# One adaLN block, two gate blocks and the compression summed on TensorE's column groups

## The chip, the cores and the metric

The kernel runs on 1 core of a Trainium2 chip. The metric is the device time of one execution, in microseconds (us). Engines are called PE (TensorE, its weight loads PEld), DVE (VectorE), ACT (ScalarE), POOL (GpSimd) and SP (SyncE, which here only starts DMAs). Each has its own in-order queue of instructions.

## The reference, cut to what matters

One layer over 256 tokens of width 4096. What the change touches is the vector-matrix product `mod` and the function `compress`:

```
mod = c @ w_ada[l] + b_ada[l]                      # c: 4096, w_ada: 4096 x 12288
shift, scale, gate = jnp.split(mod, 3, axis=-1)
u = x * (1.0 + scale[:, None]) + shift[:, None]
proj = u @ w_in[l]                                 # 256 x 4096 times 4096 x 11824
...
def compress(k, pe, w1, w2):                       # k: kc or vc, 256 tokens, 2 groups of 128
    blk = k[:, cmp_idx] + pe[:, None, :]           # 15 windows of 32 tokens, stride 16
    blk = ...reshape(B, n_cmp, G, CMP_LEN * D)     # 32 * 128 = 4096 inputs
    return jax.nn.silu(blk @ w1) @ w2              # w1: 4096 x 256, w2: 256 x 128
...
y = jnp.concatenate([y_rg, y_nsa, y_hg], axis=-1) @ w_out[l]
x = _layer_norm(ALPHA * x + (1.0 + gate[:, None]) * y, ln_g[l], ln_b[l])
```

Between `proj` and `y` stand three groups of heads: a gated recurrence (rg), sparse attention with compressed, selected and window branches (nsa), and a gated linear recurrence in chunks (hg).

## The kernel before, in words

All weights are float32 and are streamed once from HBM, in tiles of 128 x 1024 (512 KB). PE multiplies the large matrices as three products of rounded parts (a weight tile `raw` is split into `hi` on ACT and `lo` = raw - hi on DVE and POOL), lines 457 (input projection, "win" steps) and 969 (output projection, "wout" steps). Small products are made from unrounded float32 operands; each of these stands in the trace as two passes through PE.

**Stages.** The 4096 inputs are cut into ten blocks of 2, 2, 2, 3, 3 and five times 4 tiles of 128. For each block, `mod` has to be there for the block's rows (scale and shift), and then its rows of `w_in` are multiplied. So the order is: sum adaLN block 0; then for each block kb its win steps, while the chunks of adaLN block kb+1 arrive and are summed. In the last block's win steps the heads' values become complete, and the heads' own work begins. After them come the wout steps, in three parts; the first part needs for each of its 8 column blocks the head pairs 0 to 3 (rg) and 12 (hg), in this order.

**The sum of an adaLN or gate block.** A chunk is 128 partitions x 2 rows x 512 columns, from tile pool `raw`/`hi`/`lo`/`ra` (four buffers each; after the start only `ra`). `ada_sum` (line 352) takes the oldest chunk and for each of its rows lets DVE do ps = raw * c + ps on 128 x 512 (two instructions). At the block's end ACT copies ps to SBUF and PE sums over the partitions with a product with ones (`ada_end` line 395 for scale and shift, `gate_end` line 414 for a gate block of 512 columns). There are ten adaLN blocks and eight gate blocks, numbered NKB to NKB+7; the gate blocks fall due from the last win block on to the wout steps. In the start stage every third chunk of block 0 (5 of 16) is summed by PE instead (`ada_on_pe`, line 368, products at 375): the 128 x 128 piece of the chunk is the weight and one column of c moves, 8 products for a chunk. After block 0 PE runs N_IDLE = 8 idle products (line 1219).

**The compression.** 16 steps "cmp", one in between the win steps of the last block: 8 for kc, then 8 for vc. A step holds 4 of the 32 tokens of a window; for each it makes 2 products (line 511) with a 128 x 128 piece of w1 as weight and 30 moving columns (15 windows x 2 groups). ACT and DVE then make the silu of the sum (`post`).

**What sets the order.** A planner in the kernel writes the order of every engine's queue. It goes through the steps; background work ("fibers": the heads, gate ends, constants) is advanced by `run_bg` (line 1177), one stage of each fiber per call. In the last win block and after it, `run_bg` is called twice in a step: after the first part of the step's products (line 1255 and after) and at its end. `Meter` counts what each of DVE, ACT and POOL owes; `lapse` pays off HALF = 1.28 us for each call; fibers wait while DVE or ACT owes over MAY_OWE. Heads run in lanes of 2 (rg) and 3 (hg, nsa); the hg lane opens when all rg fibers have been started, the nsa lane when all hg fibers have been. When a wout step needs a head pair that isn't written yet, the planner calls `run_bg` again and again until that fiber is complete: all fiber instructions it writes meanwhile stand in the queues ahead of that step. An hg fiber (line 668) goes through seven levels, L = 1 to 64: four small products (line 708), whose result DVE puts into a matrix with copy_predicated, while DVE and POOL scale q and k for the next level.

Of the kernel before, what the change touches and what calls it, by code (L numbers as in the profile page):

```python
# [11 lines left out]
FT = mybir.dt.float32  # L12
# [6 lines left out]
P = 128  # L19
# [115 lines left out]
def trunk(ctx: ExitStack, tc: tile.TileContext, pack, xT, xz, w_ada, b_row, w_in, w_out, rg_w, w1, w2,  # L135
# [68 lines left out]
    def late_consts():  # L204
# [20 lines left out]
        late["cb"] = cb  # L225
        vm = consts.tile([P, 1], FT, name="vm")
# [112 lines left out]
    def ada_begin(b):  # L339
        _, w, m = ADA[b]  # L340
        ada_state[b] = [ps_x() for _ in range(0, w, 512)]

# [9 lines left out]
    def ada_sum():  # L352
        _, b, i, raw, _ = pending.pop(0)
        _, w, m = ADA[b]
        acc = ada_state[b]
        for j in range(m):
            c_ = vec("c", i * m + j)
            for q, ps in enumerate(acc):
                r_ = raw[:, j, q * 512:min(w, (q + 1) * 512)]
                n = r_.shape[-1]  # L360
                if i == 0 and j == 0:
                    dve.tensor_scalar(ps[:, :n], r_, c_, None, op0=OP.mult)
                else:
                    dve.scalar_tensor_tensor(ps[:, :n], r_, c_, ps[:, :n], op0=OP.mult, op1=OP.add)
        if b >= NKB and i == NKT // m - 1:
            fibers.append([gate_end(b - NKB), 1, 0, 0, tick[0] + GATE_WAIT])

    def ada_on_pe(raw, first):

        _, w, m = ADA[0]  # L370
        if first:
            ada_state["pe"] = ps_x()
        for j in range(m):
            for q in range(w // P):
                nc.tensor.matmul(ada_state["pe"][:, q:q + 1], lhsT=raw[0][:, j, q * P:(q + 1) * P],
                                 rhs=vec("c", raw[1] * m + j), start=first and j == 0 and q == 0,
                                 stop=False, skip_group_check=True)

    def ada_end(kb, xt=None):
# [13 lines left out]
        pp = ada_state.pop("pe") if kb == 0 else ps_x()  # L393
        for q in range(2 * n):
            nc.tensor.matmul(pp[:, q:q + 1], lhsT=acc[q], rhs=ones[:, 0:1],  # L395
                             start=kb > 0, stop=True, skip_group_check=kb == 0)
# [103 lines left out]
    def cmp_step(which, c):  # L500
# [3 lines left out]
        def mm():  # L504
# [3 lines left out]
            for i in range(4):  # L508
                l = 4 * c + i
                for hf in range(2):  # L510
                    nc.tensor.matmul(s_["ph"][:, hf * 256:hf * 256 + 2 * N_CMP],
                                     lhsT=st.raw[:, i * 256 + hf * P:i * 256 + (hf + 1) * P],
                                     rhs=s_["kpe"][l // 16][:, l % 16].rearrange("p a b -> p (a b)"),
                                     start=(l == 0 and hf == 0), stop=(l == CMP_LEN - 1 and hf == 1),
                                     skip_group_check=True)
                if i == 1:
                    yield
# [4 lines left out]
        def post():  # L522
# [3 lines left out]
            h_ = consts.tile([P, 2, 2 * N_CMP], FT, name=f"cmp_h{which}")  # L526
            sg = strm.tile([P, 2, 256], FT, name=nm("ev"), tag="ev", bufs=2)
            ph = s_["ph"].rearrange("p (a b) -> p a b", a=2)[:, :, :2 * N_CMP]
            act.activation(sg[:, :, :2 * N_CMP], ph, AF.Sigmoid)
            dve.tensor_mul(h_, ph, sg[:, :, :2 * N_CMP])  # L530
            ps_free()
            drop(2)
            s_["h"] = h_
            done.add(("cmp_h", which))

        st.work.append((mm, post))
        return st

    def cmp_prep(which):
# [4 lines left out]
        for a in range(2):  # L544
            t_ = slot("kpe", [P, 16, 2, N_CMP])
            for g in range(2):
                dve.tensor_add(t_[:, :, g], kv[:, :, g, a:a + N_CMP],
# [679 lines left out]
    for i in range(N):  # L1227
# [94 lines left out]
ON_PE = 3  # L1322
N_IDLE = 8
# [89 lines left out]
```

## Time and profile before

| | us |
|---|---|
| median of 3 runs (lowest, highest) | 1651.84 (1648.28, 1655.22) |
| profiled execution, its own time | 1653.54 |
| its span, first to last instruction | 1651.7 |
| PE busy in the span | 1601.7 (97%), 11800 matmuls |
| PEld, weight loads | 1503.8 (91%) |
| DVE busy | 1327.6 (80%) |
| ACT, POOL busy | 971.5 (59%), 953.7 (58%) |
| DMA read | 485.12 MB, 296 GB/s over the span |

How to read it: a matmul's time in the trace reaches from its start to the end of its run through the array, and several are under way at once. So PE is shown busy even where matmuls start further apart than they could; how far apart they start is the better measure, and a wait shows in the chain of waits or as a stretch with fewer matmuls than the time would allow.

### The profile page before, as it was taken

The page shows a single profiled execution, that of the slowest core. Times are in us where ns is not written, and L with a number is a line of the kernel's source. Part 1 is how long each engine was busy: PE and PEld are TensorE (multiplying, and loading weights), DVE is VectorE, ACT ScalarE, POOL GpSimd, SP SyncE. Part 2 cuts the span into 40 slices and gives each one's busy share as a digit, 9 for nine tenths or more (in the row PEclk, how much of TensorE's full clock was granted, in tenths as well). Part 3 has the DMA queues.
Part 4 walks back from the last instruction along what each step waited for, and adds up shares of the span by engine and source line. Part 5 has one row for each costly group of instructions (what it writes and reads, how often), then busy time and mean ns, then how long its engine had stood idle before and what let it go on. Part 6 is the DMA issues. An engine that isn't in the chain of part 4 may idle for free.

```text
span 1651.7 us, 33249 instructions
## 1 busy us (share of the span) xinstructions
PE 1601.7 (97%) x11800; PEld 1503.8 (91%) x11800; DVE 1327.6 (80%) x2297; ACT 971.5 (59%) x1557; POOL 953.7 (58%) x765
## 2 busy tenths in 40 slices
PE   7999999998999999999999999889999999999997
PEld 7999999998999999999999998889988888878884
DVE  5778988799788788788787787899689688968875
ACT  3887666665655555555555566763565555655552
POOL 2579977786655555455455445567543445455555
PEclk9999999999999999999999998999999999999999
DMA  8998989998999899899898886767667766689983
GB/s 321 377 333 307 373 299 344 306 384 305 335 339 343 292 343 328 301 348 327 300 344 321 316 293 225 252 230 262 236 223 242 240 212 205 217 294 370 341 327 146
DMA packets 146486, 491.50 MB, mean 298 GB/s; under 512 B 16264, under 2 KB 17288, under 8 KB 146320
## 3 DMA queue, kind: packets, MB, share of 16 engines
q1 hardware_dynamic: 146320, 489.38, 82.8%
q8 instruction: 93, 1.52, 0.4%
q14 instruction: 73, 0.60, 0.1%
HBM read 485.12 MB, written 4.19 MB: 296 GB/s over the span
## 4 chain that ended last, share of the span: by engine, by line
PE 81%; DVE 9%; DMA 4%; ACT 3%; issue 2%; POOL 1%; SPq 0%; DVEq 0%; ACTq 0%; POOLq 0%
PE mm L457 51%; PE mm L969 21%; DVE ps L119 2%; DVE lo L119 2%; DMA raw<-in_w_in_dram 2%; DVE acc L119 2%; DMA ra<-in_w_ada_dram 1%; ACT hi L119 1%; DVE rgt L119 1%; PE ps L708 1%; PE ps L395 1%; PE ps L901 1%; PE ps L792 1%; PE ps L1296 1%; DVE hgA L119 1%
## 5 line engine op out<-in xcount | busy, mean ns | idle before, releaser
L119 POOL TENSOR_TENSOR lo<-raw,hi 128x576 fp32r<-128x576 f32 (+4 forms) x527 | 707.8, 1345 | 606.2 <-ACT hi L119 581.2
L119 ACT CAST hi<-raw 128x1024 fp32r<-128x1024 f32 (+3 forms) x527 | 528.8, 1003 | 489.2 <-POOL lo L119 230.2
L457 PE MATMUL mm<-uh,hi 128*128 128x256 f32 x2560 | 718.1, 281 | 15.7 <-DVE lo L119 13.6
L457 PE MATMUL mm<-uh,lo 128*128 128x256 f32 x2560 | 712.5, 278 | 1.7 <-DVE lo L119 1.1
L457 PE MATMUL mm<-ul,hi 128*128 128x256 f32 x2560 | 712.4, 278 | 0.0
L119 DVE SCALAR_TENSOR_TENSOR ps<-ra,pk,ps 128x512 f32<-128x512 f32 x750 | 525.2, 727 | 11.7 <-DMA ra<-in_w_ada_dram 5.8
L457 PEld LDWEIGHTS mm<-uh,hi 128*128 128x128 f32 x2560 | 484.5, 189 | 19.3 <-DVE lo L119 16.5
L457 PEld LDWEIGHTS mm<-uh,lo 128*128 128x128 f32 x2560 | 483.9, 189 | 2.1 <-DVE lo L119 1.3
L457 PEld LDWEIGHTS mm<-ul,hi 128*128 128x128 f32 x2560 | 484.7, 189 | 0.3 <-issue 0.2
L119 DVE TENSOR_TENSOR lo<-raw,ps 128x448 fp32r<-128x448 f32 (+4 forms) x500 | 303.1, 606 | 225.8 <-ACT ps L119 184.5
L119 ACT CAST ps<-raw 128x448 fp32r<-128x448 f32 (+4 forms) x500 | 259.6, 519 | 7.4 <-DVE acc L119 6.4
L119 DVE TENSOR_TENSOR acc<-mm,acc 128x512 f32<-128x512 f32 (+1 forms) x346 | 231.2, 669 | 0.0
L969 PE MATMUL mm<-hi,yh 128*128 128x512 f32 x512 | 210.8, 412 | 0.3 <-ACT ev L119 0.3
L969 PE MATMUL mm<-hi,yl 128*128 128x512 f32 x512 | 201.3, 393 | 0.0
L969 PE MATMUL mm<-lo,yh 128*128 128x512 f32 x512 | 200.1, 391 | 0.0
L969 PEld LDWEIGHTS mm<-hi,yh 128*128 128x128 f32 x512 | 96.4, 188 | 23.3 <-issue 5.7
L457 PE MATMUL mm<-hi,uh 128*128 128x256 f32 (+1 forms) x384 | 110.4, 288 | 7.1 <-ACT hi L119 3.0
L969 PEld LDWEIGHTS mm<-hi,yl 128*128 128x128 f32 x512 | 96.1, 188 | 21.5
L969 PEld LDWEIGHTS mm<-lo,yh 128*128 128x128 f32 x512 | 96.5, 188 | 19.1 <-issue 1.2
L457 PE MATMUL mm<-hi,ul 128*128 128x256 f32 (+1 forms) x384 | 108.9, 284 | 0.0
L457 PE MATMUL mm<-lo,uh 128*128 128x256 f32 (+1 forms) x384 | 108.9, 284 | 0.0
L119 POOL TENSOR_TENSOR acc<-ev,acc 128x512 f32<-128x512 f32 x77 | 101.9, 1323 | 2.4 <-ACT ev L119 2.4
(203 smaller groups left out, 1488.3 us busy)
## 6 DMA issues: line engine op xcount, KB each, us to landing
ra<-in_w_ada_dram SPq DMA_DIRECT2D x324, 512.0 KB, 5.5
raw<-in_w_in_dram SPq DMA_DIRECT2D x291, 512.0 KB, 4.8
raw<-in_w_out_dram SPq DMA_DIRECT2D x128, 512.0 KB, 4.8
raw<-in_w_in_dram SPq DMA_DIRECT2D x90, 384.0 KB, 5.3
ra<-in_w_ada_dram SPq DMA_DIRECT2D x64, 384.0 KB, 5.6
ra<-in_w_dram SPq DMA_DIRECT2D x16, 512.0 KB, 4.2
xz<-in_xz_dram SPq DMA_DIRECT2D x16, 256.0 KB, 5.8
out_dram<-z SPq DMA_DIRECT2D x16, 256.0 KB, 2.4
```

The costliest lines, as they stand in the source:

```text
L119: return f(*a, **k)
L395: nc.tensor.matmul(pp[:, q:q + 1], lhsT=acc[q], rhs=ones[:, 0:1], start=kb > 0, stop=True, skip_group_check=kb == 0)
L457: nc.tensor.matmul(dst, lhsT=l_, rhs=r_, start=s and n_ == 0, stop=e and n_ == 2)
L708: nc.tensor.matmul(pl[:, (2 * x + j) * 64:(2 * x + j + 1) * 64], lhsT=k[:, j, x * P:(x + 1) * P], rhs=qp[:, j, x * P:(x + 1) * P].rearrang ...
L792: nc.tensor.matmul(s1[:, b * T:(b + 1) * T], lhsT=q[:, j, P:], rhs=kk[b][:, g], start=True, stop=True)
L901: nc.tensor.matmul(o, lhsT=v0, rhs=eT[:, 0:2], start=b == 0, stop=False)
L969: nc.tensor.matmul(state[x], lhsT=a_, rhs=b_, start=ci == 0 and j == 0 and n_ == 0, stop=ci == len(part) - 1 and j == 1 and n_ == 2)
L1296: nc.tensor.matmul(pb, lhsT=rows[-1 - x], rhs=rows[i // 2][:, i % 2 * 512:i % 2 * 512 + 512], start=True, stop=True)
```

## The change

Adds: `sel`, a constant of 128 x 32 with ones at rows n, 32+n, 64+n and 96+n of column n. The blocks in ON_PE (adaLN block 0 and the first two gate blocks) get their accumulator set to zero by DVE, and `ada_sum` makes four products for a chunk instead of DVE's two instructions: one column of c is the weight (128 x 1) and 256 columns of the chunk move; the result is one row of 256, at partition 0, 32, 64 or 96 of the accumulator, which are TensorE's four column groups. The ends of the blocks stay as they were: the copy by ACT and the product with ones, which now sums four rows and zeros.

The compression's products are turned round in the same way: 32 columns of the windows' values are the weight (30 and two of zeros), 256 columns of w1 move, and the four tokens of a step go to the four column groups; 4 products in a step instead of 8. The four partial sums are then copied by ACT and added by two products with `sel` in a new fiber, `cmp_hidden`. The planner calls `run_bg` only once in a cmp step now. The idle products are 4 instead of 8.

```diff
+        sel = consts.tile([P, 32], FT, name="sel")
+        dve.tensor_reduce(sel, ident.rearrange("p (a m) -> p m a", a=4), axis=AX.X, op=OP.add)
...
         ada_state[b] = [ps_x() for _ in range(0, w, 512)]
+        if b in ON_PE:
+            dve.memset(ada_state[b][0], 0.0)
...
-        for j in range(m):
+        if b in ON_PE:
+
+            for j in range(2):
+                for h in range(2):
+                    o = 32 * (2 * j + h)
+                    nc.tensor.matmul(acc[0][o:o + 1, h * 256:h * 256 + 256], lhsT=vec("c", i * 2 + j),
+                                     rhs=raw[:, j, h * 256:h * 256 + 256], start=i == 0, stop=i == NKT // 2 - 1,
+                                     skip_group_check=True)
+        for j in range(m if b not in ON_PE else 0):
...
-    def ada_on_pe(raw, first):
...
-                nc.tensor.matmul(ada_state["pe"][:, q:q + 1], lhsT=raw[0][:, j, q * P:(q + 1) * P],
-                                 rhs=vec("c", raw[1] * m + j), start=first and j == 0 and q == 0,
-                                 stop=False, skip_group_check=True)
...
-                for hf in range(2):
-                    nc.tensor.matmul(s_["ph"][:, hf * 256:hf * 256 + 2 * N_CMP],
-                                     lhsT=st.raw[:, i * 256 + hf * P:i * 256 + (hf + 1) * P],
-                                     rhs=s_["kpe"][l // 16][:, l % 16].rearrange("p a b -> p (a b)"),
-                                     start=(l == 0 and hf == 0), stop=(l == CMP_LEN - 1 and hf == 1),
-                                     skip_group_check=True)
-                if i == 1:
-                    yield
+                nc.tensor.matmul(s_["ph"][32 * i:32 * i + 32, :256], lhsT=s_["kpe"][l // 16][:, l % 16],
+                                 rhs=st.raw[:, i * 256:(i + 1) * 256], start=c == 0, stop=c == 7,
+                                 skip_group_check=True)
...
+            s_["part"] = slot("part", [P, 512])
+            act.copy(s_["part"][:, :256], s_["ph"][:, :256])
             ps_free()
             drop(2)
+            fibers.append([cmp_hidden(which), 1, 0, 0, tick[0] + 1])
...
+        for hf in range(2):
+            nc.tensor.matmul(ph[:, 32 * hf:32 * hf + 32], lhsT=s_["part"][:, hf * P:(hf + 1) * P], rhs=late["sel"],
+                             start=True, stop=True)
...
-            t_ = slot("kpe", [P, 16, 2, N_CMP])
+            t_ = slot("kpe", [P, 16, 2 * N_CMP + 2])
+            dve.memset(t_, 0.0)
...
-        if i % ON_PE == ON_PE - 1:
-            raw = ada_load(0, i, tags[i])
-            ada_on_pe((raw, i), i == ON_PE - 1)
-        else:
-            ada_chunk(0, i, 0, tags[i])
-            ada_sum()
+        ada_chunk(0, i, 0, tags[i])
+        ada_sum()
...
-                    if i >= n_win0:
+                    if i >= n_win0 and st.kind != "cmp":
                         lapse(HALF)
                         run_bg()
...
-ON_PE = 3
-N_IDLE = 8
+ON_PE = 0, NKB, NKB + 1
+N_IDLE = 4
```

Three places in PE's queue show what the change does to the order. In the rows, L367 (after) is the new product of `ada_sum`, L375 (before) the old one of `ada_on_pe`; L395 and L398 are the product with ones, L1219 and L1230 the idle products, L457 and L460 the input projection.

First, PE at the end of the start stage, before:

```order
L375 MATMUL ps_97<-pk,lo_150 128x1 x8
L375 MATMUL ps_97<-pk,ra_168 128x1 x8
L395 MATMUL ps_97<-ones,aacc_182 128x1 x4
L1219 MATMUL mm_197<-ident 128x128 x8
L457 MATMUL mm_251<-uh_211,hi_186 128x256
L457 MATMUL mm_251<-ul_212,hi_186 128x256
```

And after:

```order
L367 MATMUL ps_84<-ra_172,pk 1x256 x4
L367 MATMUL ps_84<-ra_178,pk 1x256 x4
L398 MATMUL ps_195<-ones,aacc_184 128x1 x4
L1230 MATMUL mm_200<-ident 128x128 x4
L460 MATMUL mm_250<-uh_210,hi_188 128x256
L460 MATMUL mm_250<-ul_211,hi_188 128x256
```

PE sums 16 chunks there (the last two stand here) instead of 5; the 11 others leave DVE's queue, and four idle products are gone.

Second, PE around the third cmp step in the last win block, before; L511 is the compression's product:

```order
L457 MATMUL mm_14053<-uh_13532,hi_13934 128x256
L457 MATMUL mm_14053<-ul_13533,hi_13934 128x256
L457 MATMUL mm_14053<-uh_13532,lo_13935 128x256
L511 MATMUL ps_13848<-kpe_13684,ra_13968 128x30 x8
L457 MATMUL mm_14137<-uh_13489,hi_14003 128x256
```

And after; L513 is the compression's product, L630 a product of an rg fiber:

```order
L460 MATMUL mm_14063<-uh_13534,hi_13948 128x256
L460 MATMUL mm_14063<-ul_13535,hi_13948 128x256
L460 MATMUL mm_14063<-uh_13534,lo_13949 128x256
L367 MATMUL ps_13403<-ra_13911,pk 1x256 x4
L513 MATMUL ps_13864<-ra_13970,kpe_13690 32x256 x4
L630 MATMUL ps_14118<-rgy_13994,rgw_13992 128x256 x2
L630 MATMUL ps_14121<-rgy_13994,rgw_13992 128x256 x2
L367 MATMUL ps_13403<-ra_13964,pk 1x256 x4
L367 MATMUL ps_13403<-ra_13966,pk 1x256 x4
L460 MATMUL mm_14143<-uh_13491,hi_14015 128x256
```

Gate chunks (L367) now stand in PE's queue, often right beside a cmp step; there are 32 such chunks and 16 cmp steps between the win steps.

Third, PE ahead of the fifth wout step, which needs head pair 12. Before (L969 is the output projection; L756, L742 to L744, L708, L733 and L769 belong to hg fibers):

```order
L969 MATMUL mm_16065<-hi_16038,yl_15365 128x512
L756 MATMUL ps_16174<-ones,hgsq_16131 128x1 x4
L742 MATMUL ps_16180<-hgA_15321,acc_726 128x128
L743 MATMUL ps_16180<-hgA_15322,acc_726 128x128
L744 MATMUL ps_16180<-hgA_15321,acc_726 128x128
...
L708 MATMUL ps_16187<-hgqp_15324,hgk_15214 128x64 x4
L756 MATMUL ps_16209<-ones,hgsq_16199 128x1 x4
...
L969 MATMUL mm_16047<-hi_16079,yh_16235 128x512
```

And after (L984 is the output projection, L723 a level of an hg fiber, L748 to L784 its later products):

```order
L984 MATMUL mm_15913<-hi_15892,yl_15921 128x512
L723 MATMUL ps_16039<-hgqp_15788,hgk_15605 128x64 x4
L723 MATMUL ps_16057<-hgqp_15926,hgk_15835 128x64 x4
L723 MATMUL ps_16062<-hgqp_15603,hgk_15002 128x64 x4
L723 MATMUL ps_16075<-hgqp_15788,hgk_15605 128x64 x4
L723 MATMUL ps_16080<-hgqp_15603,hgk_15002 128x64 x4
L723 MATMUL ps_16089<-hgqp_15926,hgk_15835 128x64 x4
...
L748 MATMUL ps_16228<-hgqp_15926,hgk_15835 128x128 x2
L784 MATMUL ps_16232<-ident,rs_16206 128x128 x4
...
L984 MATMUL mm_15901<-hi_15932,yh_16251 128x512
```

Sixteen levels of three hg fibers stand between the fourth and the fifth wout step, where one stood before. The first product of an hg fiber comes after 8748 of the 10368 large products, and came after 8448. From the place after the 8916th on, the heads' products stand at the same large products as before.

## Rows read from the trace of the kernel before

**Rows 1.** Windows of the core: us, busy (instructions) of each engine, clock, DMA, GB/s.

```profile
core 0: us, PE busy (x) PEld busy (x) DVE busy (x) ACT busy (x) POOL busy (x), PEclk, DMA share, GB/s
440.00:960.00 520.00, 520.00 (x4538) 520.00 (x4537) 413.01 (x683) 288.32 (x400) 270.22 (x193) 1.00 0.90 326
1000.00:1166.00 166.00, 150.60 (x1173) 146.13 (x1172) 153.24 (x239) 93.42 (x143) 103.12 (x85) 0.94 0.71 249
1166.00:1632.00 466.00, 461.15 (x2258) 379.61 (x2257) 365.37 (x657) 269.78 (x484) 237.55 (x188) 1.00 0.73 254
```

**Rows 2.** Waits of PE, whole span: who waited for whom, total, times, longest.

```profile
PE mm L457 <- DVE lo L119: 17.3, 16, 5.0
PE ps L511 <- DMA ra<-in_w_dram: 2.0, 1, 2.0
```

**Rows 3.** The chain that ended last: start, duration, what.

```profile
684.46 126.74 PE mm L457 x1104
...
1147.64 2.62 PE ps L708 x24
...
1153.14 1.70 PE ps L511 x16
```

**Rows 4.** Groups of PE instructions by form, 1000 to 1166 us.

```profile
L511 PE MATMUL ps<-kpe,ra 128*128 128x30 f32 x192 | 24.1, 278 | 2.0 <-DMA ra<-in_w_dram 2.0
L708 PE MATMUL ps<-hgqp,hgk 128*128 128x64 f32 x144 | 18.4, 278 | 1.0 <-DVE hgA L119 1.0
```

**Rows 5.** Groups of DVE instructions by form, 1000 to 1166 us.

```profile
L119 DVE SCALAR_TENSOR_TENSOR ps<-ra,pk,ps 128x512 f32<-128x512 f32 x56 | 42.2, 753 | 1.1
...
L119 DVE COPY_PREDICATED hgA<-mask,ps 128x256 f32<-128x256 int32 x17 | 9.2, 539 | 0.0
L119 DVE TENSOR_TENSOR hgqp<-hgqp,acc 128x256 f32<-128x256 f32 x9 | 7.9, 878 | 0.0
```

**Rows 6.** Timeline of DVE, first instruction of the first and third gate block.

```profile
951.14 0.74 DVE L119 TENSOR_SCALAR ps<-ra,pk 128x512 f32<-128x512 f32 x1
...
1136.97 0.79 DVE L119 TENSOR_SCALAR ps<-ra,pk 128x512 f32<-128x512 f32 x1
```

**Rows 7.** Timeline of the end of the start stage.

```profile
24.13 3.57 PE L375 MATMUL ps<-pk,ra 128*128 128x1 f32 x16 [0.27 <-DMA ra<-in_w_ada_dram]
25.46 1.55 DVE L119 SCALAR_TENSOR_TENSOR ps<-ra,pk,ps 128x512 f32<-128x512 f32 x2 [0.72 <-DMA ra<-in_w_ada_dram]
27.68 1.86 PE L395 MATMUL ps<-ones,aacc 128*128 128x1 f32 x8
29.40 3.76 PE L1219 MATMUL mm<-ident 128*128 128x128 f32 x16
30.89 0.62 ACT L119 CAST uh<-xT 128x512 fp32r<-128x512 f32 x1 [1.88 <-DVE xT L119]
32.82 0.56 PE L457 MATMUL mm<-uh,hi 128*128 128x256 f32 x1
34.77 0.28 PE L457 MATMUL mm<-uh,hi 128*128 128x256 f32 x1
```

**Rows 8.** Timeline of PE around narrow and 256-column float32 products.

```profile
1343.50 0.40 PE L969 MATMUL mm<-hi,yl 128*128 128x512 f32 x1
1343.73 0.60 PE L873 MATMUL ps<-ident,lc 128*15 128x128 f32 x4
1344.09 0.48 PE L969 MATMUL mm<-hi,yh 128*128 128x512 f32 x1
1344.41 0.40 PE L969 MATMUL mm<-lo,yh 128*128 128x512 f32 x1
...
1346.94 0.59 PE L792 MATMUL ps<-acc,acc 128*128 128x256 f32 x2
1347.37 0.38 PE L793 MATMUL ps<-acc,acc 128*128 128x128 f32 x2
```

**Rows 9.** Timeline of PE ahead of the fifth wout step.

```profile
1180.98 0.95 PE L756 MATMUL ps<-ones,hgsq 128*128 128x1 f32 x8
...
1190.58 0.48 PE L969 MATMUL mm<-hi,yh 128*128 128x512 f32 x1
```

More of the change, by code (lines that the diff above doesn't have):

```diff
@@ L225, in late_consts @@
         late["cb"] = cb
+        sel = consts.tile([P, 32], FT, name="sel")
+        dve.tensor_reduce(sel, ident.rearrange("p (a m) -> p m a", a=4), axis=AX.X, op=OP.add)
+        yield 0
+        late["sel"] = sel
         vm = consts.tile([P, 1], FT, name="vm")
@@ L366, in ada_sum @@
             fibers.append([gate_end(b - NKB), 1, 0, 0, tick[0] + GATE_WAIT])
-    def ada_on_pe(raw, first):
[L370 to L374, printed above, removed]
-                nc.tensor.matmul(ada_state["pe"][:, q:q + 1], lhsT=raw[0][:, j, q * P:(q + 1) * P],
-                                 rhs=vec("c", raw[1] * m + j), start=first and j == 0 and q == 0,
-                                 stop=False, skip_group_check=True)
     def ada_end(kb, xt=None):
@@ L392, in ada_end @@
         yield 1
-        pp = ada_state.pop("pe") if kb == 0 else ps_x()
+        pp = ps_x()
         for q in range(2 * n):
             nc.tensor.matmul(pp[:, q:q + 1], lhsT=acc[q], rhs=ones[:, 0:1],
-                             start=kb > 0, stop=True, skip_group_check=kb == 0)
+                             start=True, stop=True)
         yield 0
@@ L525, in post, with cmp_hidden @@
             s_ = CMP[which]
[L526 to L530, printed above, removed]
+            s_["part"] = slot("part", [P, 512])
+            act.copy(s_["part"][:, :256], s_["ph"][:, :256])
             ps_free()
             drop(2)
-            s_["h"] = h_
-            done.add(("cmp_h", which))
+            fibers.append([cmp_hidden(which), 1, 0, 0, tick[0] + 1])
         st.work.append((mm, post))
         return st
+    def cmp_hidden(which):
+        s_ = CMP[which]
+        ph = ps_x()
+        for hf in range(2):
+            nc.tensor.matmul(ph[:, 32 * hf:32 * hf + 32], lhsT=s_["part"][:, hf * P:(hf + 1) * P], rhs=late["sel"],
+                             start=True, stop=True)
+        drop()
+        yield 0
+        h_ = consts.tile([P, 2, 2 * N_CMP], FT, name=f"cmp_h{which}")
+        sg = strm.tile([P, 2, 256], FT, name=nm("ev"), tag="ev", bufs=2)
+        act.activation(sg[:, 0, :64], ph[:, :64], AF.Sigmoid)
+        dve.tensor_mul(h_.rearrange("p a (g n) -> p (a g) n", g=2),
+                       ph[:, :64].rearrange("p (a n) -> p a n", n=16)[:, :, :N_CMP],
+                       sg[:, 0, :64].rearrange("p (a n) -> p a n", n=16)[:, :, :N_CMP])
+        ps_free()
+        s_["h"] = h_
+        done.add(("cmp_h", which))
+        yield 0
     def cmp_prep(which):
@@ L544, in cmp_prep @@
         for a in range(2):
-            t_ = slot("kpe", [P, 16, 2, N_CMP])
+            t_ = slot("kpe", [P, 16, 2 * N_CMP + 2])
+            dve.memset(t_, 0.0)
             for g in range(2):
-                dve.tensor_add(t_[:, :, g], kv[:, :, g, a:a + N_CMP],
+                dve.tensor_add(t_[:, :, 16 * g:16 * g + N_CMP], kv[:, :, g, a:a + N_CMP],
                                pe[:, 16 * a:16 * a + 16, None].to_broadcast([P, 16, N_CMP]))
```

## The prediction

> **What bounds the kernel now.** I read the views in this order: windows, waits of PE, chain, then groups and timeline of the stretches that lose time. The windows [rows 1] show three kinds of stretch. From 440 to 960 us PE is busy without a gap; the chain there is one run of 1104 large products in 126.74 us [rows 3], 0.115 us each, and nothing but PE's own work counts. From 1166 to 1632 PE is busy for 461 of 466 us. In between, from 1000 to 1166, PE has 15 us of plain gaps and a granted clock of 0.94 on average, while DVE is busy for 153 of 166 us: here DVE sets the pace. The waits agree: PE's longest total is for `lo` parts from DVE, 17.3 us [rows 2].
>
> How much that stretch loses I take from the matmul starts. It holds 1173 [rows 1], of which 192 are of the compression and 144 of hg levels [rows 4]. The chain gives 1.70/16 = 0.106 us for the first kind and 2.62/24 = 0.109 for the second [rows 3]. So PE needs 192 x 0.106 + 144 x 0.109 + 837 x 0.115 = 132 us, and some 4 for about 45 changes from one kind of product to another, at 0.09 each: after the narrow products of [rows 8] the next large start follows at 0.32 instead of 0.23. That is 136 of 166 us: **30 us are lost**.
>
> **The change part by part**, for the profiled execution's 1653.5 us.
>
> *Price of four products on four column groups.* The trace has no two products on different groups. It has the pass: a float32 product with 256 moving columns is two passes, 0.43 us together (from 1346.94 to 1347.37 in [rows 8]). A chunk, and a cmp step, is four such products, eight passes. If the groups work at the same time, that is 0.43 us; if not, 1.72. I take 0.6: the two passes, and 0.17 for the time that a pass needs to run out (it lasts 0.39 to 0.40, while the next starts after 0.23 [rows 8]). I choose the low end since the four products share neither rows of the result nor weights; this is the weakest number of the prediction.
>
> The Trainium skill, "TensorE: Matmul & The Clock Gate", Part 3, reports products on three column groups side by side at 2.38 times the speed. No row here shows this; by that factor eight passes would take about 0.72 us, an estimate, and the sum below would be 6 us higher.
>
> *Gate blocks.* Off DVE go 2 blocks x 16 chunks x 2 instructions x 0.753 us [rows 5] = 48 us. They lie between 951 and 1137 us [rows 6], even enough that 137/186 of them, 35 us, fall behind 1000, where DVE is the bound; the first 13 relieve nothing, since PE is full there. DVE's 153 us become about 118 for 166, so PE becomes the bound. Of the 30 lost us I let 6 remain for waits on single results (DMA of a cmp tile, 2.0 [rows 2], ACT): **-24**; bounds -30 and -12. On PE come 32 x 0.6 = **+19**; bounds 14 and 55. The waits for the chunks' DMAs move from DVE's queue to PE's, where large products stand behind them; the planner sums a chunk some steps after its load, so I cost this at nothing, and it is part of the 6.
>
> *Compression.* 16 steps x 1.70 us [rows 3] = 27.2 go; 16 x 0.6 = 9.6 come, with 0.9 for two times eight passes of `cmp_hidden` at 0.109 (4 products): **-17**; bounds -19 and +1. The zeroing of the window tiles and of three accumulators is under 2 us on DVE, hidden once DVE isn't the bound.
>
> *Changes of kind.* The 16 cmp places were there; 32 new places at 0.09: **+3**, less where a chunk stands beside a cmp step.
>
> The Trainium skill, "TensorEngine Tiling (Array Packing)", Key Properties, speaks against the change here: it says that going from one tiling to another drains the array. The nearest rows, products with 15 columns of weights between large ones [rows 8], start 0.23 us after the large one ahead of them, as large ones do among themselves, and cost 0.09 at their end; that is no drain on the way in. What a drain would make of the sum is a rival below.
>
> *Start.* The last chunk of block 0 is there at 25.46 us, since DVE waited until then; DVE ends at 27.01 [rows 7]. On PE it ends at about 26.1. The product with ones takes 1.86 us for 8 passes [rows 7], twice the later spacing, as do the ten large products from 32.82 to 34.77 (0.217 us apart against 0.115): I read that as the lower clock level, with one-column products ahead of it. With 256 columns moving I expect the higher one, 0.9 less in each of the two. The first large product starts at 32.82, though its operand uh was ready at 31.51; the idle products, which end at 33.16, stood in its way [rows 7], and half of them go. So it starts at about 29.9, and up to 3.8 us are gained. From about 160 to 440 us PE waited for DVE's results (about half of the 17.3 of [rows 2]), and part of such a lead may be given back there: **-2.5**; bounds -4 and, if the eight passes go one by one (16 chunks x 1.72 = 27.5 us, from about 6 on), +5.
>
> *What else moves: the hg fibers.* One call of `run_bg` less in each cmp step delays the rg fibers, and the hg lane opens 300 large products later. Its work is then written while the planner is stuck at the fifth wout step: sixteen levels of three fibers, one after the other on PE, with nothing else to run. Before, this place took 9.6 us [rows 9] for 76 passes, 8.3 us of work. After, PE has there 16 x 8 passes and 88 of the fibers' ends, 216 x 0.109 = 23.6 us, which is not new work but moved. A level needs PE 0.87, then DVE 0.54 + 0.88 [rows 5], then about 0.5 for run-out and signals, 2.8 us for a lone fiber. The third fiber has all seven levels to go: three rounds shared by three fibers, bound by DVE at 3 x 1.42 = 4.3, three by two at 2.9, one alone at 2.8, and the end, about 6 us: 30 us, 6 more than PE's work against 1.3 before. With a lower clock in the gaps I take **+7**; bounds 0 and +20 (sixteen lone levels, 45 us less 23.6). Behind the 8916th large product the order is as before, PE full, and nothing more changes.
>
> **The sum:** -24 + 19 - 17 + 3 - 2.5 + 7 = -14.5: 1639 us. The median of the runs is 1.7 below the profiled execution: **1637 us**. PE's work itself is then about 5 us more; the gain is all from what DVE no longer holds up.
>
> **The rivals.**
>
> *Pairs in order (slower).* The two passes of a product use the same group and stand beside one another in the queue. If passes start strictly in order, a second pass waits for the first of its own group, and only it and the next group's first pass overlap: five slots instead of two, 5 x 0.215 = 1.07, a chunk 1.1 us. Gates then cost 35, the compression -9: -24 + 35 - 9 + 3 - 2.5 + 7 = +9.5, or 1661. It turns slower from 0.9 us for a chunk on. Against it: nothing in the trace; for it: large products start in order everywhere. The Trainium skill, "TensorE: Matmul & The Clock Gate", Part 3, states that matmuls start and end in program order, by which this rival would hold; no run here shows it yet.
>
> *No overlap (slower).* Eight passes, 1.72 us: gates +55, compression +1, start +5: +47, 1699. For it: only the caution that no row shows two groups at work.
>
> *Drain at each change (no difference).* If PE runs empty on the way in and out, 48 places cost 2 x 0.17 instead of 0.09 for 32: 16 instead of 3, 1650. The exit's 0.09 is for it, the entry's 0.23 against it [rows 8].
>
> *The pile of hg levels eats the gain (no difference).* With +20 for that place: 1650. For it: three fibers with PE as their only queue, in the order shown above; against it: DVE is freed of the two gate blocks.
>
> **How the numbers follow.** I give the forecast 0.45, the drain 0.13, the pile 0.08, pairs in order 0.24, no overlap 0.10. What a measurement can tell from no change is about 0.5%, 8 us: under 1643.6 is faster, over 1660.1 slower. The forecast's own range is 1626 to 1648, and 0.38 of its 0.45 count as faster, 0.07 as no change. Drain and pile together: 0.04 faster, 0.15 none, 0.02 slower. Pairs: 0.06 none, 0.18 slower. No overlap: all slower. Together 0.42 faster, 0.28 same, 0.30 slower. The range runs from 1624, a little under the forecast's own, to 1668, which holds most of the pairs; no overlap stays outside, with the ends of the others.
>
> **What would show it.** In the profile after: the first passes of the four products of one chunk starting within a few hundredths of a us, and 0.6 us from one chunk to what follows (1.1: pairs; 1.7: no overlap); cmp steps at 0.6 instead of 1.70; the first large product at about 30 us, and the ones product at 0.106 a pass; DVE under 75% busy in the stretch up to the first wout step, and PE without gaps there; then a place of about 30 us ahead of the fifth wout step in which PE waits for DVE's hg results. I am wrong if a chunk takes over 0.9 us of PE, or if PE's gaps up to the wout steps stay although DVE is idle.

## The result

| | before | after |
|---|---|---|
| median of 8 runs each, same chip (lowest, highest) | 1656.55 (1648.28, 1660.1) | 1668.01 (1659.25, 1672.81) |
| profiled execution (span) | 1653.54 (1651.7) | 1672.81 (1671.1) |
| mean granted clock of PE | 0.992 | 0.978 |

The ratio is 1.0071, 95% interval 1.0044 to 1.0097: the changed kernel is slower by 0.7%, 11 us in the medians and 19.3 in the profiled executions. The profiled one of the changed kernel is the slowest of its eight, so about 8 of the 19.3 us are spread between executions and not the change. The forecast was 1637 and faster. Line numbers of the changed kernel: L367 the new products of `ada_sum`, L398 the product with ones, L460 the input projection, L513 the compression, L723 to L784 the hg levels and their ends, L984 the output projection.

**Where the 19.4 us of span went.** Set the two traces beside one another at five points. The ones product of the last adaLN block starts at 939.46 before and 938.83 after: -0.6. From there to the first product of the output projection it is 226.9 and 208.8 us: -18.1. From that to the fifth wout place 14.4 and 14.5. The place itself, from the last large product ahead of it to the next, is 9.84 us (1180.74 to 1190.58, [rows 9]) and 46.78: **+36.9**. From there to the end 461.1 and 462.2. So the stretch in which DVE set the pace did get shorter, and one place gave back twice as much. Most of the 18.1 is no gain, though: 140 passes of the hg fibers, 15.3 us at 0.109, stood in the stretch before and stand behind it now. The points, before:

```profile
939.46 1.84 PE L395 MATMUL ps<-ones,aacc 128*128 128x1 f32 x16
...
1166.38 0.40 PE L969 MATMUL mm<-hi,yh 128*128 128x512 f32 x1
...
1180.74 0.39 PE L969 MATMUL mm<-hi,yl 128*128 128x512 f32 x1
```

and after, where the place itself is shown further down:

```profile
938.83 1.84 PE L398 MATMUL ps<-ones,aacc 128*128 128x1 f32 x16
...
1147.65 0.48 PE L984 MATMUL mm<-hi,yh 128*128 128x512 f32 x1
```

### The profile page after: what moved, and what is told of

The parts are those of the page before. It is cut to its first block, busy times and chain, and to the rows that moved or that the text cites. A ratio compares the mean times of both kernels' runs of the same rounds, so it can differ in the third digit from the quotient of the medians.

```text
span 1671.1 us, 33513 instructions
## 1 busy us (share of the span) xinstructions
PE 1617.8 (97%) x11976; PEld 1485.1 (89%) x11976; DVE 1269.7 (76%) x2219; ACT 979.2 (59%) x1565; POOL 956.2 (57%) x765
## 5 line engine op out<-in xcount | busy, mean ns | idle before, releaser
L460 PE MATMUL mm<-uh,hi 128*128 128x256 f32 x2560 | 721.0, 282 | 16.0 <-DVE lo L119 7.5
L460 PE MATMUL mm<-ul,hi 128*128 128x256 f32 x2560 | 713.8, 279 | 0.1
L460 PE MATMUL mm<-uh,lo 128*128 128x256 f32 x2560 | 713.6, 279 | 0.0
L460 PEld LDWEIGHTS mm<-uh,hi 128*128 128x128 f32 x2560 | 485.6, 190 | 30.8 <-issue 12.3
L460 PEld LDWEIGHTS mm<-ul,hi 128*128 128x128 f32 x2560 | 485.3, 190 | 1.0 <-issue 0.5
L460 PEld LDWEIGHTS mm<-uh,lo 128*128 128x128 f32 x2560 | 484.2, 189 | 0.1
L119 DVE SCALAR_TENSOR_TENSOR ps<-ra,pk,ps 128x512 f32<-128x512 f32 (+1 forms) x682 | 474.3, 725 | 6.3 <-DMA ra<-in_w_ada_dram 1.0
L984 PE MATMUL mm<-hi,yh 128*128 128x512 f32 x512 | 210.9, 412 | 0.3 <-ACT ev L119 0.3
L984 PE MATMUL mm<-hi,yl 128*128 128x512 f32 x512 | 201.4, 393 | 0.0
L984 PE MATMUL mm<-lo,yh 128*128 128x512 f32 x512 | 200.2, 391 | 0.0
L984 PEld LDWEIGHTS mm<-hi,yh 128*128 128x128 f32 x512 | 96.5, 188 | 23.1 <-issue 5.7
L984 PEld LDWEIGHTS mm<-hi,yl 128*128 128x128 f32 x512 | 96.2, 188 | 21.3
L460 PE MATMUL mm<-hi,uh 128*128 128x256 f32 (+1 forms) x384 | 110.1, 287 | 3.9 <-DVE lo L119 2.6
L984 PEld LDWEIGHTS mm<-lo,yh 128*128 128x128 f32 x512 | 96.6, 189 | 19.0 <-issue 1.2
L460 PE MATMUL mm<-hi,ul 128*128 128x256 f32 (+1 forms) x384 | 108.4, 282 | 0.0
L460 PE MATMUL mm<-lo,uh 128*128 128x256 f32 (+1 forms) x384 | 108.4, 282 | 0.0
```

The source lines that it names most:

```text
L119: return f(*a, **k)
L460: nc.tensor.matmul(dst, lhsT=l_, rhs=r_, start=s and n_ == 0, stop=e and n_ == 2)
L984: nc.tensor.matmul(state[x], lhsT=a_, rhs=b_, start=ci == 0 and j == 0 and n_ == 0, stop=ci == len(part) - 1 and j == 1 and n_ == 2)
```

## The profile after

The windows that answer to [rows 1] (busy us and instructions of PE, PEld, DVE, ACT, POOL; then PE's granted clock, DMA share and GB/s):

```profile
core 0: us, PE busy (x) PEld busy (x) DVE busy (x) ACT busy (x) POOL busy (x), PEclk, DMA share, GB/s
440.00:960.00 520.00, 520.00 (x4540) 518.86 (x4540) 409.72 (x678) 286.58 (x397) 268.53 (x191) 1.00 0.90 327
1000.00:1166.00 166.00, 151.64 (x1269) 131.48 (x1267) 115.80 (x179) 113.07 (x170) 104.69 (x82) 0.97 0.79 282
1166.00:1632.00 466.00, 462.65 (x2226) 386.50 (x2227) 361.44 (x660) 257.93 (x468) 228.04 (x180) 0.96 0.69 240
```

From 440 to 960 nothing has changed. From 1000 to 1166 DVE is down from 153.24 to 115.80 us, the number that was forecast (118), but PE still has 14 us of gaps. That the number came out is in good part luck: in `turns_back` (below), where the hg work stays in this window, DVE is busy for 137.65 us, so up to 22 of the 37 us are work that moved behind the window. In the third window PE is as busy as it was and does less with it: the clock is 0.96 instead of 1.00. Cut finer, the low clock has one home:

```profile
1160.00:1170.00 10.00, 7.44 (x54) 6.90 (x52) 8.44 (x19) 1.53 (x2) 5.67 (x7) 0.87 0.59 200
1170.00:1180.00 10.00, 10.00 (x48) 10.00 (x48) 7.05 (x16) 0.00 (x0) 4.85 (x6) 0.50 0.00 0
1180.00:1190.00 10.00, 10.00 (x49) 10.00 (x48) 4.50 (x12) 1.55 (x3) 3.03 (x5) 0.50 0.08 28
1190.00:1200.00 10.00, 9.01 (x43) 8.82 (x42) 2.97 (x8) 3.09 (x5) 4.31 (x5) 0.50 0.00 0
1200.00:1210.00 10.00, 10.00 (x51) 9.83 (x50) 1.97 (x5) 3.21 (x7) 3.28 (x4) 0.58 0.00 0
1210.00:1220.00 10.00, 10.00 (x55) 8.31 (x54) 4.34 (x7) 8.62 (x15) 3.33 (x3) 1.00 0.43 134
```

For 40 us PE counts as busy, with one gap of 1 us, nearly all of it at the lower of its two levels, 1.2 GHz, and DMA has almost come to rest, while no wout step uses up a tile. The timeline of PE shows the way in and the way out (start, duration, and in brackets the idle time before it), and answers to [rows 9]:

```profile
1162.12 0.39 PE L984 MATMUL mm<-hi,yl 128*128 128x512 f32 x1
1162.35 2.79 PE L723 MATMUL ps<-hgqp,hgk 128*128 128x64 f32 x24
1165.92 1.10 PE L723 MATMUL ps<-hgqp,hgk 128*128 128x64 f32 x8 [0.78 <-POOL hgk L119]
1168.80 1.52 PE L723 MATMUL ps<-hgqp,hgk 128*128 128x64 f32 x6 [1.78 <-DVE hgA L119]
...
1208.90 0.47 PE L984 MATMUL mm<-hi,yh 128*128 128x512 f32 x1
```

and the chain that ended last gives the price of a pass on either level (start, duration, what):

```profile
1153.41 1.73 PE ps L723 x16
...
1168.80 10.48 PE ps L723 x48
...
1180.24 3.31 PE ps L723 x16
```

1.73/16 = 0.108 us before the fall, 3.31/16 = 0.207 after it. Two gaps for POOL's and DVE's results come first, and within the second the clock falls. From there on a level takes so long on PE that DVE's and POOL's share of it is hidden: but for 0.9 us at 1198 the chain is PE alone, at half speed, to 1208.90.

Four products on four column groups are what the forecast took them for. In the start stage, where PE waited for a chunk, four passes start within 0.02 us (the other four of the chunk at 22.32 to 22.34), and in the stretch a chunk, a cmp step and the next product follow at 0.43 and 0.54:

```profile
22.11 0.40 PE L367 MATMUL ps<-ra,pk 128*1 128x256 f32 x4 [0.63 <-DMA ra<-in_w_ada_dram]
...
994.62 0.28 PE L460 MATMUL mm<-uh,lo 128*128 128x256 f32 x1
994.83 0.61 PE L367 MATMUL ps<-ra,pk 128*1 128x256 f32 x8
995.26 0.61 PE L513 MATMUL ps<-ra,kpe 128*32 128x256 f32 x8
995.80 0.70 PE L630 MATMUL ps<-rgy,rgw 128*128 128x256 f32 x2
```

The eight passes run as two rounds of four; in which order they stand in the queue, the trace doesn't show. The place of a cmp step, 1.70 us in [rows 3], is 0.54 now, and a chunk costs 0.43 to 0.54. The chunk starts 0.21 us after the large product ahead of it, where large products follow one another at 0.115; with this way in, a lone chunk between large products takes 0.64 (0.21 + 0.54 - 0.115).

The start answers to [rows 7]:

```profile
26.43 0.61 PE L367 MATMUL ps<-ra,pk 128*1 128x256 f32 x8 [0.61 <-DMA ra<-in_w_ada_dram]
27.75 1.86 PE L398 MATMUL ps<-ones,aacc 128*128 128x1 f32 x8 [0.71 <-ACT aacc L119]
29.47 2.05 PE L1230 MATMUL mm<-ident 128*128 128x128 f32 x8
31.66 0.58 PE L460 MATMUL mm<-uh,hi 128*128 128x256 f32 x1
...
37.46 0.38 PE L460 MATMUL mm<-uh,hi 128*128 128x256 f32 x1
37.68 0.29 PE L460 MATMUL mm<-ul,hi 128*128 128x256 f32 x1
```

The first large product comes 1.2 us earlier (31.66 for 32.82), but the last chunk is there at 26.43 only, not at 25.46, the ones product is as slow as it was (1.86 for 8), and the large products run at 0.21 apart until 37.46, not 34.77: the lead is gone before the second block. The clock had been at the higher level during the last chunks, and fell just ahead of the ones product:

```profile
20.60:27.40 6.80, 3.12 (x44) 0.53 (x40) 0.00 (x0) 0.29 (x1) 0.00 (x0) 1.00 1.03 418
27.50:37.60 10.10, 9.58 (x41) 8.99 (x42) 4.30 (x9) 7.02 (x12) 5.65 (x4) 0.50 0.58 200
```

## The experiments

Ratios are to the kernel before on the same chip, with 95% intervals. "Lost" is a window's length less PE's busy time multiplied by the granted clock, from the two windows 940 to 1160 (the stretch) and 1160 to 1240 (the wout place) of each profiled execution. The clock is given to 0.01, so a difference of 1 us or so says nothing. Before in the stretch, and after in both:

```profile
940.00:1160.00 220.00, 204.38 (x1623) 199.17 (x1622) 194.62 (x305) 131.47 (x201) 128.93 (x105) 0.95 0.74 257
...
940.00:1160.00 220.00, 204.54 (x1732) 177.10 (x1733) 145.74 (x226) 145.15 (x217) 128.70 (x98) 0.97 0.79 282
1160.00:1240.00 80.00, 76.45 (x398) 71.11 (x397) 45.66 (x95) 30.92 (x57) 35.44 (x35) 0.74 0.32 109
```

| kernel | ratio | lost in stretch | lost at place |
|---|---|---|---|
| before | 1 | 25.8 | 0.7 |
| after | 1.0071 [1.0044, 1.0097] | 21.6 | 23.4 |
| turns_back | 0.9964 [0.9946, 0.9982] | 16.7 | 0.5 |
| before_fewer_turns | 1.0158 [1.0107, 1.0210] | 27.8 | 13.9 |
| filler | 1.0008 [0.9990, 1.0026] | 17.7 | 2.0 |
| gates_on_dve | 1.0175 [1.0134, 1.0215] | 47.2 | 13.4 |
| turns_gates_dve | 1.0029 [1.0015, 1.0042] | 43.8 | 1.7 |
| turns_old_cmp | 1.0042 [1.0023, 1.0061] | 9.4 | 0.3 |
| turns_four_gates | 1.0038 [1.0025, 1.0051] | 15.7 | 0.0 |
| turns_idle8 | 0.9940 [0.9922, 0.9958] | 14.7 | 0.5 |
| idle8_one_gate | 1.0036 [1.0022, 1.0050] | 33.3 | 3.1 |
| idle8_rg_apart | 1.0078 [1.0058, 1.0097] | 25.3 | 12.3 |
| idle8_rg_one | 1.0060 [1.0035, 1.0084] | 19.4 | 20.5 |

In this measure a matmul's whole time in the trace counts as work, so it shows a stretch of many short runs too full. The prediction counted starts (its 30 us are those of 1000 to 1166). Done so from the last ones product to the first wout product (1200 large products at 0.115, the old compression's 256 passes at 0.106, a chunk or a new cmp step at 0.43, all others at 0.109; the price of changes of kind and of the low clock stays in what is lost), this estimate gives 37 lost us of 226.9 before, 40 of 208.8 after, 37 of 226.4 in `turns_back`, 60 of 231.5 in `turns_gates_dve` and 25 of 233.8 in `turns_old_cmp`. Both measures agree on which kernel loses most and least; that the stretch loses less after the change than before shows in the first alone.

### The pile: turns_back and before_fewer_turns

`turns_back` is the changed kernel with `run_bg` called twice in a cmp step again; `before_fewer_turns` is the kernel before with only that call taken out.

```diff
-                    if i >= n_win0 and st.kind != "cmp":
+                    if i >= n_win0:
```

> The changed kernel, with the planner's first call of background work in a cmp step put back; all products as changed. In its queue the sixteen hg levels ahead of the fifth wout step are gone (two small products of fiber ends are left there). Theory 1 (the loss is the pile of hg levels, which the planner's missing turns made, and PE's low clock in it): that place falls from 46.7 to under 10 us, some 13 to 15 us of hg products go back between the win steps, and the execution takes about 1645 to 1652, at or below before. Rival (the new products on PE, or gate chunks waiting in PE's queue, cost the time): within 5 us of the changed kernel, about 1668.

> The kernel before with one edit alone: no first call of background work in a cmp step. No product is changed. Its queue gets a pile of 100 small products ahead of the fifth wout step. Theory 1: slower than before by 15 to 25 us, with a low clock in the pile. Rival: within 5 us of before.

One line holds the whole loss, both ways: put back, the changed kernel is faster than the one before, by 0.36%; taken out of the kernel before, that is slower by 1.6%, 25 us. (In the spans of its profile the stretch is 15 us shorter, the place 27 longer, and 12 more come behind the place, which is not explained.) In `turns_back` the largest distance between two large products at the wout steps is 4.02 us (46.78 in the changed kernel); in `before_fewer_turns` it is 37.29, for over half of it at the same low clock:

```profile
1180.00:1190.00 10.00, 9.95 (x47) 9.65 (x47) 5.68 (x12) 1.01 (x3) 3.51 (x4) 0.50 0.00 0
```

So the sixteen calls are what starts the hg lane in time, and the loss has nothing to do with column groups.

### The clock in the pile: filler

The changed kernel with one more product of 256 columns (the identity as weight, into columns of the accumulator that nobody reads) in each hg level that is written while a wout step is held up. It only adds work.

```diff
+            if stuck[0]:
+                nc.tensor.matmul(pl[:, 256:512], lhsT=ident, rhs=v[:, 0], start=True, stop=True)
```

> The changed kernel with one more product for each hg level that is written while a wout step is held up (identity times 256 columns, into unused columns of the level's own accumulator, read by nobody): 15 to 16 products, 32 passes, more work. If the pile is long because PE's clock falls there: the passes start 0.11 instead of 0.21 us apart, the place takes 30 to 38 us instead of 46.7, the total falls by 8 to 15. If it is long because each level waits for DVE and POOL: the place grows by the added passes, 3 to 7 us, and the total with it.

The place is 33.29 us with the added work and 46.78 without; the ratio falls from 1.0071 to 1.0008. PE does 83 passes in 10 us instead of 48:

```profile
1170.00:1180.00 10.00, 10.00 (x83) 9.74 (x82) 7.13 (x18) 1.70 (x4) 5.25 (x7) 1.00 0.09 28
```

By the windows the low clock takes 76.45 x 0.26 = 20 us between 1160 and 1240 in the changed kernel, about half of the place's excess, and nothing here. The rest is the levels' own work and its round trips. The 15 added products take 0.48 us each, so at the higher level the place would take about 26 us without them, an estimate: the 9.84 of before, 15.3 for the 140 passes that moved here, and 1. What isn't separated is by which of two ways they kept the clock up: they are wider, and they fill PE's waits (the longest is 0.99 us here, 1.78 in the changed kernel).

### Gates and compression, with the pile and without: gates_on_dve, turns_gates_dve, turns_old_cmp

`gates_on_dve` is the changed kernel, and `turns_gates_dve` is `turns_back`, each with the two gate blocks summed by DVE (the first adaLN block stays on PE). `turns_old_cmp` is `turns_back` with the compression's code of before.

```diff
-ON_PE = 0, NKB, NKB + 1
+ON_PE = 0,
```

> The changed kernel with the two gate blocks summed by DVE again; block 0, the compression and the planner's turns as changed; the pile stays in the queue. If DVE was the bound of the last win block, as predicted, this is slower than the changed kernel by 5 us or more, and the first wout step comes later than its 1147.7 us by as much. If freeing DVE gains nothing there, the first wout step comes at the same time or up to 14 us earlier (32 chunks of 0.43 us less on PE) and the total is the same or lower.

> The changed kernel with the planner's turns put back and its two gate blocks summed by DVE again (the first adaLN block stays on TensorE): the compression's worth without the pile, and, against the kernel with the turns alone (0.9964 of before), the gates' worth. Theory A, DVE sets the pace of the stretch before the first wout step, so that PE work taken out there comes to nothing: first wout product at 1163 to 1167 as before, ratio 0.998 to 1.002, and the gates on PE are worth about 0.3%. Theory B, the compression's 17 us count in full and the gates on PE bring nothing: first wout product at about 1150, ratio 0.990, faster than with the gates on PE. Theory C, the gates on PE are worth the 17 to 20 us that they are worth beside the pile (1.0175 against 1.0071): ratio 1.007, first wout product at about 1180.

> The kernel with the turns put back, and with the compression of before (16 steps of eight passes by turns of 15 to 30 columns, 1.70 us each, in place of 0.47): the new compression's worth beside the gates on PE. Theory A, with the gates off DVE PE bounds the stretch, so the 20 us that return to PE are paid in full: ratio about 1.008, first wout product at about 1183. Theory B, chains of results (hi, lo and acc from ACT, POOL and DVE, a weight tile's DMA) set the stretch and PE has idle time to take the compression in: ratio 0.997 to 1.001, first wout product at 1166 to 1172.

Beside the pile the gates on PE are worth 17 us (1.0175 to 1.0071; 9 by the spans of the profiled executions, and the first wout product comes 8.4 us later without them, at 1156.07, as the expectation had it for DVE as the bound); without it 11 (1.0029 to 0.9964). The two changes without the pile make a square:

| | compression of before | new compression |
|---|---|---|
| gates on DVE | 1 | 1.0029 |
| gates on PE | 1.0042 | 0.9964 |

(All but the first have block 0 on PE and four idle products, and the kernel with that start and neither change was not run; so what each is worth alone, apart from the start, is not shown.) With either one alone the kernel is slower than the one before; with both it is faster. None of the theories gave both numbers: the first wout product comes at 1170.16 and 1175.34, between the theories' places. The windows from 940 to 1160 say why, in the order `turns_gates_dve`, `turns_old_cmp`, `turns_back`:

```profile
940.00:1160.00 220.00, 189.47 (x1473) 173.64 (x1474) 192.40 (x303) 130.16 (x198) 128.59 (x104) 0.93 0.74 253
```

```profile
940.00:1160.00 220.00, 214.91 (x1866) 195.76 (x1865) 156.92 (x242) 129.07 (x196) 133.84 (x105) 0.98 0.71 254
```

```profile
940.00:1160.00 220.00, 207.44 (x1814) 179.81 (x1813) 167.09 (x258) 134.94 (x206) 136.10 (x108) 0.98 0.74 264
```

With the gates on DVE the new compression frees PE for nothing: DVE is busy for 192 of 220 us, PE's lost time rises from 25.8 to 43.8. PE then even waits for the compression's tiles:

```profile
PE ps L513 <- DMA ra<-in_w_dram: 11.9, 4, 4.2
PE mm L460 <- DVE lo L119: 8.9, 9, 3.3
```

With the old compression the gates on PE find it nearly full: 9.4 us lost of 220, and their passes are paid for. Together, one makes the room that the other fills.

### How many gate blocks: turns_four_gates, idle8_one_gate

```diff
-ON_PE = 0, NKB, NKB + 1
+ON_PE = 0, NKB, NKB + 1, NKB + 2, NKB + 3
```

> The kernel with the turns put back and four gate blocks on PE instead of two: 32 more chunks of 0.45 us on PE (14 us), 48 us less on DVE. Theory A, DVE still bounds part of the stretch (18 to 19.6 of 20 us busy from 1080 to 1160): ratio 0.988 to 0.994. Theory B, chains of results set the stretch and DVE's load no longer matters: 14 us more work in a stretch with some 12 us of idle PE, and chunks later than 1166 where PE is full: ratio 0.998 to 1.005.

> The kernel with the turns put back, eight idle products, and one gate block on TensorE in place of two (16 chunks, 7 us less on PE, 24 us more on DVE). With none of them the ratio was 1.0029 with half the idle products, with two 0.9964, with four 1.0038. Theory A, DVE's load decides below two blocks and PE's work above: one block lies between none and two, 0.996 to 1.000. Theory B, one block is relief enough: 0.989 to 0.993, since PE saves 7 us.

Four blocks: theory B. DVE falls to 160 us of 220, the lost time stays (15.7 for 16.7), and the 12 us that it is slower than `turns_back` are about the 14 of the added passes. One block: the direction of theory A, beyond its range, no better than none: 33.3 us are lost, 18.6 more than with two (`turns_idle8`), for 24 us of instructions put back on DVE. Of none, one, two and four, two is the fastest; why one block loses so much is not shown.

### The start: turns_idle8

```diff
-N_IDLE = 4
+N_IDLE = 8
```

> The kernel with the turns put back and eight idle products at the start instead of four. The forecast's step on the start: the idle products stand ahead of the first large product, so four more cost up to 2 us, of which little is left by 939: ratio 0.9964 to 0.998. The rival: they run while the first operand is waited for anyway, and more of them bring the high clock sooner (large products were 0.21 apart until 37.46): first large products 0.12 apart earlier, 1 to 2 us gained at the start, ratio 0.995 to 0.9964.

The rival was right in the mechanism; the ratio lies a little under its range. The idle products stand in the way for about 1 us, but the high clock comes back sooner. The timeline of PE:

```profile
29.34 3.76 PE L1230 MATMUL mm<-ident 128*128 128x128 f32 x16
32.75 0.56 PE L460 MATMUL mm<-uh,hi 128*128 128x256 f32 x1
...
34.39 0.30 PE L460 MATMUL mm<-ul,hi 128*128 128x256 f32 x1
34.53 0.28 PE L460 MATMUL mm<-uh,lo 128*128 128x256 f32 x1
```

The first large product starts 1.1 us later than in the changed kernel, and the products are 0.12 apart from 34.4 on, not from 37.7: the ones product of the second block is at 88.59 instead of 90.85 and the last one at 936.43. This is the fastest kernel of the study, 0.6% under the one before. Its interval overlaps with that of `turns_back`; that eight idle products are better than four rests on the trace's start more than on the medians. There the eleven traces with the new start agree: the clock is back at the higher level for good at 32.6 to 35.7 us in the four with eight idle products, and at 36.1 to 37.9 in the seven with four. Of that, 1.3 us are left at the second block's ones product (on average 88.6 and 89.9, with overlapping ranges). By the last one, at 936 to 946 and 936 to 942, no lead stands clear of the scatter.

### What is left in the stretch: idle8_rg_apart, idle8_rg_one

`turns_idle8`, with the rg fibers begun at least 24 turns apart, or one at a time.

```diff
-LANES = (2, 3, 3, 1)
-STAGGER = (0, 0, 8, 0)
+LANES = (1, 3, 3, 1)
+STAGGER = (24, 0, 8, 0)
```

(`idle8_rg_one` changes the first line, `idle8_rg_apart` the second.)

> The kernel with the turns put back and eight idle products (0.9940 of before), and each rg fiber begun at least 24 turns after the one before it; before, two of them ran side by side. What it asks is why the stretch still loses about 11 us of 80 between 1000 and 1080 though DVE has been freed of two gate blocks. Theory A, two rg fibers side by side fill DVE there (34 of 40 us busy from 1005 to 1045, with no gate sums in it), so that lo and acc come late: with them apart PE is idle for under 4 us from 1000 to 1080, ratio 0.987 to 0.991, unless the hg levels that open later are piled up at the wout steps. Theory B, the loss is in chains of single results from ACT and POOL, which come in any order of the fibers: ratio 0.992 to 0.997.

> The same kernel with one rg fiber at a time. Theory A (two rg fibers side by side fill DVE from 1005 to 1045): PE idle under 4 us from 1000 to 1080, ratio 0.987 to 0.991. Theory B (chains of ACT and POOL): 0.992 to 0.997. Either way the hg lane opens later, and if over some 10 us of hg levels land ahead of a wout step the ratio goes over 1.

Both theories miss; what came true is the condition that both texts named, the pile. From 1000 to 1080 PE's gaps are 9.3 us in `turns_idle8`, 7.2 with the fibers apart and 5.1 with one at a time: less, not under 4. But the later rg fibers open the hg lane later, and the pile is back, in part at the low clock (35.48 us between two large products with the fibers apart, 17.23 and 29.42 at two places with one at a time). What makes the remaining gaps there stays open; PE's waits in it are single ones:

```profile
PE mm L460 <- DVE lo L119: 5.4, 3, 3.2
PE mm L460 <- POOL lo L119: 1.4, 2, 1.2
PE ps L630 <- DMA rgw<-in_rg_w_dram: 1.2, 1, 1.2
```

## Why the prediction was wrong, step by step

- **Four products side by side: right**, and on the cheap side: 0.43 to 0.54 us for eight passes where 0.6 was taken. The times of pairs in order (1.1) and of no overlap (1.72) are refuted by that, and by the four passes that start together at 22.11. The Trainium skill ("TensorE: Matmul & The Clock Gate", Part 3) states that matmuls start and end in program order. These starts don't speak against it, since the rival's other premise, that a product's two passes stand beside one another in the queue, is shown by no trace here.
- **Changes of kind, +3: too small by up to 3 us.** A chunk starts 0.09 us later after a large product than a large one would (0.21 for 0.115), and after a cmp step the next product starts 0.11 later than its passes take (0.54 for 0.43). That is 0.2 for a place, between the 0.09 of the sum and the 0.34 of the drain rival. PE doesn't run empty: the large product that starts at 994.62 lasts until 994.90, by the trace's modelled end, and the chunk starts at 994.83.
- **Gate blocks, -24 and +19: the sizes held, where they could act.** Beside the new compression the relief measured 43.8 - 16.7 = 27 us of lost time (23 by the starts), and the chunks cost about 14 (32 x 0.43 to 0.45; up to 20 with the ways in and out).
- **Compression, -17: held in part, in the one case.** Beside the gates on PE it is worth 13 us (1.0042 to 0.9964); beside the gates on DVE, nothing. (Its "two times eight passes of `cmp_hidden`" are eight in all, as its 0.9 us has them.)
- **The step that failed in the stretch: "Of the 30 lost us I let 6 remain".** The same lost time was spent twice. Taking 17 us off PE where DVE sets the pace makes lost time (37 us to 60 by the starts, from before to `turns_gates_dve`), and the relief of DVE first pays for that (60 back to 37 in `turns_back`). Measured by the windows, the stretch lost 25.8 us before, 21.6 after, 16.7 in `turns_back`; by the starts, as the prediction had its 30, it lost 37, 40 and 37, no less than before. From the ones product to the first wout product it was 18.1 shorter, of which about 15 is hg work that moved into the pile (216 - 76 = 140 passes of 0.109, the prediction's own count): some 3 us of gain where -19 was forecast. In a sum over two engines that wait for one another, each term holds only for the state that the others leave.
- **The step that failed at the wout steps: the pile's "+7; bounds 0 and +20".** Place and mechanism were as told: the hg lane opened later, and its levels were written while the fifth wout step was held up; the 216 passes there were counted right. Its price was 36.9 - 15.3 = 21.6 us (15.3 for the 140 passes that are not new), over the upper bound. The prediction priced passes at 0.109 and let PE wait for DVE; in the trace PE waited 3.6 us in all there, and the passes were 0.207 apart. "A lower clock in the gaps" was in the text and not in the sum: the lower level came with the first two gaps and stayed, and by the windows it is 20 of the 21.6 us. The rival built on this mechanism named 1650 for a price of +20; it had nothing for a stretch that gains only 3.
- **Start, -2.5: wrong in cause, -0.6 in size**, and -0.6 is within the scatter (935.7 to 941.6 in the seven traces with this start). The clock was at the higher level while the last chunks' 256 columns moved, and at the lower one again for the ones product; the last chunk came 1 us later than taken; and of the idle products only their place in the way was counted, about 1 us, not what they do for the clock ahead of the large ones.
- **What would show it** told the cases apart: DVE at 70% and PE's gaps still there was named as a sign of error, and it was one.

The forecast's sum without the pile is -21.5; `turns_back`, which has no pile, is 0.36% faster, 6 us. The 16 us between them are, by the starts and as an estimate: the relief and the changes of kind together, which brought about 1 us and not 21; the start, 2.5; and against them 8 us by which the chunks (14 for 19) and the cmp steps (0.43 for 0.6) were cheaper. What block 0 on PE is worth by itself, no run shows.

## What to carry to other kernels

When two engines set the pace of a stretch by turns, don't add the worth of a relief of each: write down what each needs after both changes, and ask what single waits are left when neither is full. When a change touches how often a planner turns to its background work, look for the place where that work piles up at the next hard need, and price it at the clock that TensorE has there, not at the one before. One line of the planner cost more here (1.1 and 1.6%) than the whole change brought without it (0.4 to 0.6%).

## What the hardware did that was not expected

Four float32 products on four column groups cost as much as one: eight passes start as two rounds of four, end within 0.61 us and let the next product start 0.43 us after the first, where one product of two passes took 0.43 [rows 8]. And PE can be shown busy almost without a gap and run at half clock for 40 us (0.50 from 1170 to 1200), with the small products of the pile, of 1 to 128 columns; with products of 256 columns added among them the granted clock was 1.00. At the start the granted clock differs between traces of one and the same queue: in the seven with four idle products the higher level came and went between 16.3 and 27.4 us in five, and did not come before the idle products in two.
